# Compression weights with both parts side by side: one 512-column product per row of weights

## The chip, the cores and the metric

The kernel runs on one core of a Trainium2 chip. The metric is the device time of one execution in microseconds (us). The profile of one execution gives the busy time of the engines: PE (TensorE matmuls; PEld its weight loads), DVE (VectorE), ACT (ScalarE), POOL (GpSimd) and SP (SyncE, which issues the loads).

## The reference

A decoder trunk of two layers on 256 positions of 2048 features, all in float32: first a layer of dilated sliding-window attention, then a layer of sparse attention with compressed, selected and sliding-window branches, each followed by a squared-ReLU MLP and a gated per-layer embedding. What matters here is the compression that the second layer's first branch needs. Windows of 32 positions, 16 apart (15 of them), of the raw keys and the raw values of 4 groups go through a small MLP:

```python
def compress_blocks(blocks, pe, w1, w2):
    """blocks: (B, n_cmp, L, G, dh) -> (B, n_cmp, G, dh) via MLP with intra-block position enc."""
    B, n, L, G, dh = blocks.shape
    z = (blocks + pe[None, None, :, None, :]).transpose(0, 1, 3, 2, 4).reshape(B, n, G, L * dh)
    return jax.nn.gelu(z @ w1) @ w2
```

With L = 32 and dh = 128, `w1` is 4096 x 256, once for keys and once for values; there are 15 x 4 rows of `z` (padded to 64).

## The kernel before, in words

All weights stream from HBM once, in chunks of 128 partitions x 1024 float32 (512 KB), 873 of them in a fixed order. A chunk goes through three steps before PE uses it. `load` (L186) brings it into one of 4 `raw` buffers by a DMA on SP. `copy` (L198) rounds it on ACT to the matmul's reduced format, into a `whi` tile of 6. `sub` (L204) subtracts that on DVE from the raw chunk and keeps the rest as `wlo`, one of 5. A product with both parts is then nearly a full float32 product. Activations are split into two parts in the same way.

`Program` holds the steps in order; `Program.run` writes out each engine's instructions by hand in this order for chunk `at`: loads as far as `raw` buffers go (a buffer is free when the chunk four earlier has been subtracted), the copy of chunk `at + 4`, the subtraction of chunk `at + 3`, one step of each generator that is under way (`advance`), and then the chunk's matmuls. Each engine runs its instructions in that order. So on ACT the copy of chunk n+1 stands ahead of anything issued with the subtraction of chunk n.

The stage around the change comes after the key and value projections (`raw_quad`, `key_quad`). `compress("k")` has 8 chunks of `w_c1`, and `both` zips them with the 8 chunks of `value_unit("vs")`: compression chunk, value chunk, and so on. Then `compress("v")` is zipped with `value_unit("vw")`. That makes 32 chunks, from about 1388 to 1450 us.

- A chunk of `value_unit` (through `token_major`, L418 to L420) is 12 products of 512 columns.
- A compression chunk holds 4 x 128 rows of `w1`, 256 columns each. `z` (its two parts beside each other: 2 x 4 groups x 16 windows = 128 columns) is the stationary operand; it meets the 256 columns of `whi` (L938) and then of `wlo` (L939). All go into one accumulator of 128 x 256, whose upper and lower 64 rows belong to the two parts of `z`.
- `z_group` makes `z` for two chunks at a time: sums on DVE (`zf`, L914), rounding on ACT (L919), the rest on DVE (L922).
- `gelu` follows the eighth chunk. ACT copies the accumulator to `et` (L949). PE adds upper and lower rows with the stationary operand `pair`, two identities under each other (L955, a float32 matmul). Squares, tanh, transposes (L973) and the second weight (L989, L1018) come after, in steps between the next chunks.

In the value half DVE and ACT also split the next layer's activations (`xa`, L293 and L297). After the stage come one chunk of gate weights (`w_g`) and the query chunks (`w_q`, L327 and L329).

Of the kernel before, what the change touches and what calls it, by code (L numbers as in the profile page):

```python
# [10 lines left out]
F32 = mybir.dt.float32  # L11
# [4 lines left out]
P = 128  # L16
D = 2048
T = 256
# [23 lines left out]
def f32(ap):  # L42
    return ap.bitcast(F32)


class Program:
# [9 lines left out]
        self.steps, self.active, self.waiting, self.after = [], [], [], []  # L56

    def op(self, fn):
        self.steps.append((None, fn))

    def chunk(self, src, fn):
        self.steps.append((src, fn))

    def collect(self, fn):
        kept, self.steps = self.steps, []
# [32 lines left out]
            pass  # L98

    def run(self, load, copy, sub):  # L100
        srcs = [s for s, _ in self.steps if s is not None]
        raw, hi, lo = {}, {}, {}
        loaded = at = copied = subbed = 0
        for src, fn in self.steps:
            if src is None:
                g = fn()
                if g is not None:
                    self.begin(g)
                continue
            starting = at < KT // 2  # L110
            if starting:
                self.advance()
            ahead = max(0, min(SPLIT_AHEAD, at - KT // 2 + 2))
            while loaded < len(srcs) and loaded <= at + DMA_AHEAD:
                if loaded >= RAW_BUFS and loaded - RAW_BUFS >= subbed:
                    break
                raw[loaded] = load(loaded, srcs[loaded])
                loaded += 1
            while copied < loaded and copied <= at + ahead + (ahead > 0):
                hi[copied] = copy(copied, raw[copied])  # L120
                copied += 1
            while subbed < copied and subbed <= at + ahead:
                lo[subbed] = sub(subbed, raw.pop(subbed), hi[subbed])
                subbed += 1
            if not starting:
                self.advance()
            self.waiting += fn(hi.pop(at), lo.pop(at)) or []
            self.finish_tensor()
            at += 1
        self.until(lambda: not self.active and not self.waiting)  # L130
# [3 lines left out]
def kernel(ctx: ExitStack, tc: tile.TileContext, a: dict, out: bass.AP):  # L134
    nc = tc.nc
    ctx.enter_context(tc.manual_schedule())
    prog = Program()
# [4 lines left out]
    tmp = ctx.enter_context(tc.tile_pool(name="tmp", bufs=2))  # L142
# [15 lines left out]
    def bank():  # L158
        return pspool.tile([P, 512], F32, tag="mm", name="mm", bufs=4)
# [14 lines left out]
    pair = const.tile([P, 64], F32, name="pair")  # L174
# [16 lines left out]
    def pieces(n):  # L191

        return [slice(0, CH // 2), slice(CH // 2, CH)] if n < 2 else [slice(0, CH)]

    def copy(n, t):
        hi = wpool.tile([P, CH], F32R, tag="hi", name="whi", bufs=HI_BUFS)
        for c in pieces(n):
            nc.scalar.copy(hi[:, c], t[:, c])  # L198
        return hi

    def sub(n, t, hi):
        lo = wpool.tile([P, CH], F32R, tag="lo", name="wlo", bufs=LO_BUFS)
        for c in pieces(n):
            nc.vector.tensor_sub(lo[:, c], t[:, c], f32(hi)[:, c])  # L204
        return lo
# [700 lines left out]
    def z_group(n, b):  # L906

        prog.until(lambda: ready.get("r" + n) == GB)
        raw, pe, z = zt["r" + n], zt["pe_" + n], zt["z", b % 2]
        zf = cur["C"].tile([P, GB, 15, 8], F32, tag="zf", name="zf", bufs=2)  # L910
        part = list(raw.ap[0])
        win = bass.AP(tensor=raw.tensor, offset=raw.offset + 8 * b, ap=[part, [T, GB], [16, 15], [1, 8]])
        for g in range(GB):
            nc.vector.tensor_add(zf[:, g], win[:, g],  # L914
                                 pe[:, None, 8 * b:8 * b + 8].to_broadcast([P, 15, 8]))
        yield
        h4, l4 = (z[:, :, i].rearrange("p l g n -> p g n l")[:, :, :15, :] for i in range(2))
        for g in range(GB):
            nc.scalar.copy(h4[:, g], zf[:, g])  # L919
        yield  # L920
        for g in range(GB):
            nc.vector.tensor_sub(l4[:, g], zf[:, g], f32(h4[:, g]))  # L922
        ready["z", n, b] = True

    def compress(n, ring, then):

        st = []
        for c in range(8):
            def step(hi, lo, c=c):
                b = c // 2  # L930
                prog.until(lambda: ("z", n, b) in ready)
                z = zt["z", b % 2]
                if c == 0:
                    st.append(ring()[:, :256])
                for i in range(4):
                    zl = z[:, 4 * (c % 2) + i].rearrange("p a g n -> p (a g n)")
                    cols = slice(i * 256, (i + 1) * 256)
                    nc.tensor.matmul(st[0], zl, hi[:, cols], start=c == 0 and i == 0, stop=False)  # L938
                    nc.tensor.matmul(st[0], zl, lo[:, cols], start=False, stop=c == 7 and i == 3)  # L939
                return [gelu(n, st[0])] if c == 7 else []  # L940
            prog.chunk(a["w_c1"][(0 if n == "k" else 8) + c], step)
            if c % 2 == 1:
                m, b = (n, c // 2 + 2) if c < 5 else (then, c // 2 - 2)
                if m:
                    prog.op(lambda m=m, b=b: z_group(m, b))

    def gelu(n, ps):
        s = tmp.tile([P, T], F32, tag="et", name="et", bufs=7)
        nc.scalar.copy(s, ps)  # L949
        yield  # L950
        if n == "k":
            yield
        yield "tensor"
        y = bank()[:64, :256]
        nc.tensor.matmul(y, pair, s, start=True, stop=True)  # L955
        yield
        t = tmp.tile([64, T], F32, tag="et", name="et", bufs=7)
        u = tmp.tile([64, T], F32, tag="et", name="et", bufs=7)
        nc.scalar.activation(t, y, AF.Square)
        yield  # L960
        nc.vector.tensor_scalar(t, t, 0.044715, 1.0, op0=ALU.mult, op1=ALU.add)
        nc.vector.tensor_mul(t, y, t)
        yield
        nc.scalar.activation(t, t, AF.Tanh, scale=math.sqrt(2.0 / math.pi))
        yield
        nc.vector.scalar_tensor_tensor(u, t, 1.0, y, op0=ALU.add, op1=ALU.mult)
        yield
        if n == "k":
            yield
        yield "tensor"  # L970
        ps = bank()
        for k in range(2):
            nc.tensor.transpose(ps[:, k * 64:(k + 1) * 64], u[:, k * P:(k + 1) * P], ident[:64, :64])  # L973
        yield
        if n == "k":
            uT = cur["B"].tile([P, P], F32, name="uT", tag="uT", bufs=1)
            nc.scalar.copy(uT, ps[:, :P])
        else:
            uT = cur["B"].tile([P, 8, 3, 16], F32, name="uT3")
            nc.scalar.copy(uT, ps[:, :P].rearrange("p (b n) -> p b n", n=16)[:, :, None, :]  # L980
                           .to_broadcast([P, 8, 3, 16]))
        yield
        yield "tensor"
        yield from (comp_k(uT) if n == "k" else comp_v(uT))

    def comp_k(uT):
        ps = bank()
        for k in range(2):
            nc.tensor.matmul(ps[:64, :DH], uT[:, k * 64:(k + 1) * 64], zt["w2_k"][:, k, :],  # L989
                             start=k == 0, stop=k == 1)  # L990
        yield
        kc = cur["B"].tile([64, DH], F32, name="kc")
        nc.scalar.mul(kc, ps[:64, :DH], 0.5)
        yield
        w = cur["B"].tile([64, 32], F32, name="kcr")
        nc.vector.tensor_mul(w[:, :16], kc[:, 16:32], zt["rcS"][:, :16])
        nc.vector.tensor_mul(w[:, 16:], kc[:, :16], zt["rcS"][:, 16:])
        nc.vector.tensor_mul(kc[:, :32], kc[:, :32], zt["rcC"])
        nc.vector.tensor_add(kc[:, :32], kc[:, :32], w)
        yield  # L1000
        yield
        yield "tensor"
        ps = bank()
        nc.tensor.transpose(ps[:, :64], kc, ident[:64, :64])
        yield
        for g in range(GB):
            nc.scalar.copy(kt(g, 0)[:, :16], ps[:, 16 * g:16 * g + 16])
        yield
        for g in range(GB):
            nc.vector.tensor_sub(kt(g, 1)[:, :16], ps[:, 16 * g:16 * g + 16], f32(kt(g, 0)[:, :16]))  # L1010
        ready["kc"] = True
# [28 lines left out]
    def both(f, g):  # L1040
# [4 lines left out]
    raw_quad("rk", 0)  # L1045
    raw_quad("rv", 1, {5: [lambda: z_group("k", 0)], 6: [lambda: z_group("k", 1)]})
    both(lambda: compress("k", bank, "v"), lambda: value_unit("vs", 3))
    both(lambda: compress("v", bank, None),
         lambda: value_unit("vw", 5, {c: [lambda k=k: split_x(k, G_ATTN + 1, x_a1) for k in (2 * c, 2 * c + 1)]
# [284 lines left out]
```

## Time and profile before

| | before |
|---|---|
| median of 3 runs | 2513.16 us (2512.55 to 2513.68) |
| the profiled execution: its time | 2514.11 us |
| the profiled execution: span of the profile | 2511.3 us |
| mean granted clock of TensorE | 0.999 |
| loads of 512 KB from `w_c1` | 16, median 4.3 us from issue to landing |
| loads of 512 KB from `w_kv` | 48, median 4.3 us from issue to landing |
| matmul instructions of the compression's products (L938, L939) | 64 and 64 |

A row of the timeline has the start in us from the span's start, the length, engine, line, operation, result and operands, their shape, the number of instructions merged (x2), and in brackets the idle time before with what ended it. A merged row's length runs from the first start to the last end. PE's lengths overlap, since matmuls are pipelined: PE's pace is read from start to start. Rows of groups have busy time, mean length in ns, and the idle time ahead of them with its releasers. SPq rows are issues of loads.

### The profile page before, as it was taken

How to read it: one execution, taken by the hardware profiler on the slowest of the kernel's cores; microseconds unless marked ns; L12 is line 12 of the kernel's file. 1: busy time of each engine (PE TensorE's matmuls, PEld its weight loads, DVE VectorE, ACT ScalarE, POOL GpSimd, SP SyncE). 2: the span in 40 equal slices, each digit the busy share in tenths (PEclk: the TensorE clock that was granted, in tenths of full speed). 3: DMA queues.
4: the chain of work that ended last, by engine and by line, in shares of the span. 5: the costliest groups of instructions: out<-in, count | busy, mean ns of one | idle time of the engine just before them, and what ended most of it. 6: DMA issues, size and time to landing. Idle time of an engine off the chain costs nothing.

```text
span 2511.3 us, 36082 instructions
## 1 busy us (share of the span) xinstructions
PE 2500.4 (100%) x13497; PEld 2156.5 (86%) x13497; DVE 1662.3 (66%) x2808; ACT 1351.0 (54%) x2168; POOL 10.4 (0%) x24
## 2 busy tenths in 40 slices
PE   9999999999999999999999999999999999999998
PEld 8888888888888888888888889888888888888887
DVE  7766677865465565566787989766546556556676
ACT  6444444554454453455564788755545445445455
POOL 0000000000000000000000000000000000000000
PEclk9999999999999999999999999999999999999999
DMA  7555545556555655555565753455555655665553
GB/s 272 172 179 178 175 161 181 173 188 193 193 188 193 191 192 193 192 192 185 186 195 189 243 163 121 141 191 190 192 192 188 193 192 192 193 192 190 182 189 121
DMA packets 130111, 466.10 MB, mean 186 GB/s; under 512 B 14608, under 2 KB 15888, under 8 KB 129936
## 3 DMA queue, kind: packets, MB, share of 16 engines
q1 hardware_dynamic: 129264, 462.68, 56.6%
q8 instruction: 105, 1.72, 0.3%
q0 software_dynamic: 528, 1.07, 0.2%
q14 instruction: 70, 0.57, 0.1%
q10 hardware_dynamic: 144, 0.07, 0.0%
HBM read 461.65 MB, written 2.10 MB: 185 GB/s over the span
## 4 chain that ended last, share of the span: by engine, by line
PE 99%; DVE 0%; DMA 0%; SPq 0%; ACT 0%; issue 0%; DVEq 0%
PE mm L327 22%; PE at L327 17%; PE mm L329 11%; PE at L329 9%; PE mm L418 6%; PE mm L420 6%; PE mm L419 6%; PE at L420 5%; PE at L418 5%; PE at L419 5%; PE at L1180 0%; PE at L718 0%; PE mm L1204 0%; PE mm L938 0%; PE mm L939 0%; DMA raw<-in_w_v 0%
## 5 line engine op out<-in xcount | busy, mean ns | idle before, releaser
L204 DVE TENSOR_TENSOR wlo<-raw,whi 128x1024 fp32r<-128x1024 f32 (+1 forms) x875 | 1065.7, 1219 | 634.3 <-PE at L420 131.5
L198 ACT CAST whi<-raw 128x1024 fp32r<-128x1024 f32 (+1 forms) x875 | 919.8, 1052 | 880.4 <-PE at L327 198.9
L327 PE MATMUL mm<-xa,whi 128*128 128x512 f32 x2176 | 756.4, 396 | 0.0
L329 PE MATMUL mm<-xa,wlo 128*128 128x256 f32 x2176 | 587.9, 278 | 0.0
L327 PE MATMUL at<-xa,whi 128*128 128x512 f32 x1648 | 573.7, 393 | 0.0
L327 PEld LDWEIGHTS mm<-xa,whi 128*128 128x128 f32 x2176 | 401.4, 188 | 85.1 <-issue 0.4
L329 PE MATMUL at<-xa,wlo 128*128 128x256 f32 x1648 | 458.5, 278 | 0.0
L329 PEld LDWEIGHTS mm<-xa,wlo 128*128 128x128 f32 x2176 | 409.4, 188 | 9.7
L327 PEld LDWEIGHTS at<-xa,whi 128*128 128x128 f32 x1648 | 308.7, 187 | 70.0
L329 PEld LDWEIGHTS at<-xa,wlo 128*128 128x128 f32 x1648 | 310.2, 188 | 0.1
L418 PE MATMUL at<-whi,h 128*128 128x512 f32 x512 | 199.5, 390 | 0.0
L418 PE MATMUL mm<-whi,h 128*128 128x512 f32 x512 | 199.4, 389 | 0.0
L419 PE MATMUL mm<-whi,h 128*128 128x512 f32 x512 | 199.2, 389 | 0.0
L420 PE MATMUL mm<-wlo,h 128*128 128x512 f32 x512 | 199.2, 389 | 0.0
L420 PE MATMUL at<-wlo,h 128*128 128x512 f32 x512 | 199.2, 389 | 0.0
L419 PE MATMUL at<-whi,h 128*128 128x512 f32 x512 | 199.2, 389 | 0.0
L420 PEld LDWEIGHTS at<-wlo,h 128*128 128x128 f32 x512 | 96.1, 188 | 20.0
L420 PEld LDWEIGHTS mm<-wlo,h 128*128 128x128 f32 x512 | 96.1, 188 | 20.0
L418 PEld LDWEIGHTS mm<-whi,h 128*128 128x128 f32 x512 | 96.1, 188 | 19.9
L419 PEld LDWEIGHTS at<-whi,h 128*128 128x128 f32 x512 | 96.1, 188 | 19.8
L418 PEld LDWEIGHTS at<-whi,h 128*128 128x128 f32 x512 | 96.1, 188 | 19.8
L419 PEld LDWEIGHTS mm<-whi,h 128*128 128x128 f32 x512 | 96.1, 188 | 19.6
(315 smaller groups left out, 2529.5 us busy)
## 6 DMA issues: line engine op xcount, KB each, us to landing
raw<-in_w SPq DMA_DIRECT2D x512, 512.0 KB, 3.6
raw<-in_w_qk SPq DMA_DIRECT2D x96, 512.0 KB, 3.5
raw<-in_w_gate SPq DMA_DIRECT2D x56, 512.0 KB, 4.0
raw<-in_w_kv SPq DMA_DIRECT2D x48, 512.0 KB, 4.3
raw<-in_w_v SPq DMA_DIRECT2D x46, 512.0 KB, 3.6
raw<-in_w_q SPq DMA_DIRECT2D x32, 512.0 KB, 4.4
raw<-in_w_oB SPq DMA_DIRECT2D x32, 512.0 KB, 3.5
raw<-in_w_oA SPq DMA_DIRECT2D x16, 512.0 KB, 3.5
```

The lines of the kernel that those rows point to most:

```text
L198: nc.scalar.copy(hi[:, c], t[:, c])
L204: nc.vector.tensor_sub(lo[:, c], t[:, c], f32(hi)[:, c])
L327: nc.tensor.matmul(ps, hi[:, col:col + P], rhs, start=first, stop=False)
L329: nc.tensor.matmul(ps[:, :T], lo[:, col:col + P], rhs[:, :T], start=False, stop=last)
L418: nc.tensor.matmul(st[j], xh, wh, start=k == 0, stop=False)
L419: nc.tensor.matmul(st[j], xl, wh, start=False, stop=False)
L420: nc.tensor.matmul(st[j], xh, wl, start=False, stop=k == KT - 1)
```

## The change

A compression chunk is split into two other tiles. Of a chunk's four rows of weights, `whi` takes the first two with both parts side by side (256 columns rounded, 256 columns rest, twice), `wlo` the other two likewise. One product of 512 columns per row of weights then goes into an accumulator of 128 x 512, whose two halves belong to the two parts of the weights. `chunk` gets a width for such chunks (256), which `run` hands to `copy` and `sub`. `copy` makes the rounded part of the first tile; `sub` makes the rounded part of the second on ACT, and then both rests on DVE, each instruction 512 elements. `gelu` copies both halves of the accumulator (two copies of 256 columns on ACT) and adds all four quarters with two `pair` matmuls into one accumulator. All other chunks are split as before.

```diff
-                hi[copied] = copy(copied, raw[copied])
+                hi[copied] = copy(copied, raw[copied], wide[copied])
...
-                lo[subbed] = sub(subbed, raw.pop(subbed), hi[subbed])
+                lo[subbed] = sub(subbed, raw.pop(subbed), hi[subbed], wide[subbed])
...
+    def beside(t, raw, j, w):
+
+        return raw.rearrange("p (j i c) -> p j i c", j=2, c=w)[:, j], t.rearrange("p (i a c) -> p i a c", a=2, c=w)
+
+    def copy(n, t, wide):
         hi = wpool.tile([P, CH], F32R, tag="hi", name="whi", bufs=HI_BUFS)
+        if wide:
+            src, dst = beside(hi, t, 0, wide)
+            nc.scalar.copy(dst[:, :, 0, :], src)
+            return hi
...
+    def sub(n, t, hi, wide):
         lo = wpool.tile([P, CH], F32R, tag="lo", name="wlo", bufs=LO_BUFS)
+        if wide:
+            halves = [beside(both, t, j, wide) for j, both in enumerate((hi, lo))]
+            src, dst = halves[1]
+            nc.scalar.copy(dst[:, :, 0, :], src)
+            for src, dst in halves:
+                nc.vector.tensor_sub(dst[:, :, 1, :], src, f32(dst[:, :, 0, :]))
+            return lo
...
-            def step(hi, lo, c=c):
+            def step(*both, c=c):
...
-                    st.append(ring()[:, :256])
+                    st.append(ring())
                 for i in range(4):
                     zl = z[:, 4 * (c % 2) + i].rearrange("p a g n -> p (a g n)")
-                    cols = slice(i * 256, (i + 1) * 256)
-                    nc.tensor.matmul(st[0], zl, hi[:, cols], start=c == 0 and i == 0, stop=False)
-                    nc.tensor.matmul(st[0], zl, lo[:, cols], start=False, stop=c == 7 and i == 3)
+                    nc.tensor.matmul(st[0], zl, both[i // 2][:, i % 2 * 512:(i % 2 + 1) * 512],
+                                     start=c == i == 0, stop=c == 7 and i == 3)
...
     def gelu(n, ps):
-        s = tmp.tile([P, T], F32, tag="et", name="et", bufs=7)
-        nc.scalar.copy(s, ps)
+        s = [tmp.tile([P, T], F32, tag="et", name="et", bufs=7) for _ in range(2)]
+        for i in range(2):
+            nc.scalar.copy(s[i], ps[:, i * T:(i + 1) * T])
...
-        nc.tensor.matmul(y, pair, s, start=True, stop=True)
+        for i in range(2):
+            nc.tensor.matmul(y, pair, s[i], start=i == 0, stop=i == 1)
```

More of the change, by code (lines that the diff above doesn't have):

```diff
@@ L58, in op, with chunk @@
     def op(self, fn):
-        self.steps.append((None, fn))
-    def chunk(self, src, fn):
-        self.steps.append((src, fn))
+        self.steps.append((None, fn, None))
+    def chunk(self, src, fn, wide=None):
+        self.steps.append((src, fn, wide))
     def collect(self, fn):
@@ L100, in run @@
     def run(self, load, copy, sub):
-        srcs = [s for s, _ in self.steps if s is not None]
+        srcs = [s for s, _, _ in self.steps if s is not None]
+        wide = [w for s, _, w in self.steps if s is not None]
         raw, hi, lo = {}, {}, {}
         loaded = at = copied = subbed = 0
-        for src, fn in self.steps:
+        for src, fn, _ in self.steps:
             if src is None:
@@ L193, in pieces @@
         return [slice(0, CH // 2), slice(CH // 2, CH)] if n < 2 else [slice(0, CH)]
-    def copy(n, t):
+    def beside(t, raw, j, w):
+        return raw.rearrange("p (j i c) -> p j i c", j=2, c=w)[:, j], t.rearrange("p (i a c) -> p i a c", a=2, c=w)
+    def copy(n, t, wide):
         hi = wpool.tile([P, CH], F32R, tag="hi", name="whi", bufs=HI_BUFS)
+        if wide:
+            src, dst = beside(hi, t, 0, wide)
+            nc.scalar.copy(dst[:, :, 0, :], src)
+            return hi
         for c in pieces(n):
@@ L199, in copy @@
         return hi
-    def sub(n, t, hi):
+    def sub(n, t, hi, wide):
         lo = wpool.tile([P, CH], F32R, tag="lo", name="wlo", bufs=LO_BUFS)
+        if wide:
[5 more added lines that the diff above has]
+            return lo
         for c in pieces(n):
@@ L933, in step @@
                 if c == 0:
-                    st.append(ring()[:, :256])
+                    st.append(ring())
                 for i in range(4):
                     zl = z[:, 4 * (c % 2) + i].rearrange("p a g n -> p (a g n)")
-                    cols = slice(i * 256, (i + 1) * 256)
-                    nc.tensor.matmul(st[0], zl, hi[:, cols], start=c == 0 and i == 0, stop=False)
-                    nc.tensor.matmul(st[0], zl, lo[:, cols], start=False, stop=c == 7 and i == 3)
+                    nc.tensor.matmul(st[0], zl, both[i // 2][:, i % 2 * 512:(i % 2 + 1) * 512],
+                                     start=c == i == 0, stop=c == 7 and i == 3)
                 return [gelu(n, st[0])] if c == 7 else []
-            prog.chunk(a["w_c1"][(0 if n == "k" else 8) + c], step)
+            prog.chunk(a["w_c1"][(0 if n == "k" else 8) + c], step, 256)
             if c % 2 == 1:
```

## The prediction

> **What bounds the kernel now.** I read the page's top, its chain of work, then the same stage in the windows view, in the waits and in the timeline.
>
> ```profile
> span 2511.3 us, 36082 instructions
> PE 2500.4 (100%) x13497; PEld 2156.5 (86%) x13497; DVE 1662.3 (66%) x2808; ACT 1351.0 (54%) x2168; POOL 10.4 (0%) x24
> PE 99%; DVE 0%; DMA 0%; SPq 0%; ACT 0%; issue 0%; DVEq 0%
> ...
> 1388.40:1418.30 29.90, 29.81 (x162) 25.68 (x161) 26.64 (x51) 19.49 (x31) 0.00 (x0) 1.00 0.77 248
> 1418.30:1448.00 29.70, 29.70 (x161) 24.38 (x160) 29.40 (x56) 26.63 (x49) 0.00 (x0) 1.00 0.80 261
> ```
>
> TensorE is the bound: 99% of the chain that ended last is PE. So an edit gains only by giving PE less to do, and loses as soon as PE waits. The two window rows are the stage that is edited: the compression of the keys, then that of the values, each zipped chunk by chunk with a value unit. Columns are length, then busy time of PE, PEld, DVE, ACT, POOL, then clock, DMA share and GB/s. PE still never idles there (29.81 of 29.90, 29.70 of 29.70), at full clock, but everything that feeds it is near its limit: in the second half DVE has 0.3 us free of 29.70, ACT 3.1 us.
>
> ```profile
> SPq L186 <- DVE wlo L204: 31.3, 18, 4.3
> ...
> ACT whi L198 <- DMA raw<-in_w_kv: 7.4, 8, 1.8
> ...
> PEld mm L955 <- ACT et L949: 0.4, 1, 0.4
> ```
>
> These are the waits between 1388 and 1452 us (total, times, longest). Loads wait for DVE (18 times), ACT waits for loads (8 times): with four `raw` buffers this is a ring. A load starts when the subtraction of the chunk four earlier is done, ACT copies what has landed, DVE subtracts, the next load starts. The last row is where the ring already touches PE: the value side's `pair` matmul (L955) waits for ACT.
>
> **The products.** 128 products of 256 columns become 64 of 512.
>
> ```profile
> 1392.43 0.29 PE L938 MATMUL mm<-whi,z 128*128 128x256 f32 x1
> ...
> 1393.39 0.39 PE L418 MATMUL at<-whi,xa 128*128 128x512 f32 x1
> ...
> 1396.14 0.29 PE L938 MATMUL mm<-whi,z 128*128 128x256 f32 x1
> ...
> 1403.57 0.29 PE L938 MATMUL mm<-whi,z 128*128 128x256 f32 x1
> ```
>
> A compression chunk takes PE 1393.39 − 1392.43 = 0.96 us for 8 products of 256, that is 0.120 each; the 12 products of 512 of the next value chunk take 1396.14 − 1393.39 = 2.75, 0.229 each. Four wide ones are 0.92: columns count, not instructions. Saved: 16 × 0.04 = 0.64 us at the very most. [...] Two chunk pairs take PE 1403.57 − 1396.14 = 7.43 us here; that is the pace the ring must keep.
>
> **The splits.** The compression's `hi` tile now takes weight columns 0 to 511, both parts side by side, `lo` the other 512. ACT makes two copies of 512 in place of one of 1024, DVE two subtractions of 512 in place of one.
>
> ```profile
> L204 DVE TENSOR_TENSOR wlo<-raw,whi 128x1024 fp32r<-128x1024 f32 x871 | 1063.1, 1222 | 632.9 <-PE at L420 131.5 <-PE mm L420 130.0 <-PE mm L329 119.4
> L198 ACT CAST whi<-raw 128x1024 fp32r<-128x1024 f32 x871 | 917.4, 1054 | 879.0 <-PE at L327 198.9 <-PE mm L419 198.0 <-PE mm L327 196.3
> ...
> L204 DVE TENSOR_TENSOR wlo<-raw,whi 128x512 fp32r<-128x512 f32 x4 | 2.6, 691 | 1.5 <-ACT whi L198 1.4
> L198 ACT CAST whi<-raw 128x512 fp32r<-128x512 f32 x4 | 2.4, 617 | 1.3 <-DMA raw<-in_w_v 1.3
> ```
>
> DVE: 2 × 0.691 − 1.222 = +0.16 us per compression chunk; ACT: 2 × 0.617 − 1.054 = +0.18. The destinations are now runs of 256 with gaps, which no row shows; I take the price of the plain 512, since nothing in it but the step of the address differs. Two back to back may overlap a little at their ends, so +0.08 to +0.16 for DVE.
>
> The order matters more than the size. The second copy is issued with the subtraction, and the program issues the copy of chunk n+1 before the subtraction of chunk n. So on ACT it stands behind `whi` of the next chunk, and that waits for its load. On DVE the second subtraction waits for this copy, and behind it stand the value chunk's `wlo`, `zf` and `z`; SP's next loads wait for those. One turn of the ring, two chunk pairs long, from the end of a value chunk's `wlo`:
>
> ```profile
> 1396.97 0.33 SPq L186 DMA_DIRECT2D raw<-in_w_kv  x1
> ...
> 1401.78 1.05 ACT L198 CAST whi<-raw 128x1024 fp32r<-128x1024 f32 x1 [0.68 <-DMA raw<-in_w_kv]
> ...
> 1412.44 0.33 SPq L186 DMA_DIRECT2D raw<-in_w_kv  x1
> ...
> 1417.24 1.05 ACT L198 CAST whi<-raw 128x1024 fp32r<-128x1024 f32 x1 [0.90 <-DMA raw<-in_w_kv]
> ...
> 1390.06 2.00 ACT L198 CAST whi<-raw 128x1024 fp32r<-128x1024 f32 x2
> ...
> 1410.06 2.35 DVE L204 TENSOR_TENSOR wlo<-raw,whi 128x1024 fp32r<-128x1024 f32 x2
> ```
>
> - `wlo` ends 1410.06 + 2.35 = 1412.41, the load goes out 1412.44: 0.03
> - issue to the start of `whi`: 4.81 and 4.80, both with ACT waiting for the DMA: 4.80
> - two `whi` in a row take 2.00, so the second copy starts 2.00 − 1.05 = 0.95 after
> - the second copy itself 0.62, a hand-over of 0.03 as at the load
> - the second subtraction 0.69; then the value chunk's `wlo`, 2.35 − 1.22 = 1.13 further on
>
> Sum 8.25 us per turn against PE's 7.43: the ring falls behind by 0.82. Between the end of the first copies and the stage's middle there are 8 pairs, 4 turns: 3.3 us. Before the change the own copy of a chunk was enough, and the two subtractions ran without that wait.
>
> A start-up lag comes first. `whi` of the second chunk starts at 1390.06; today the compression chunk's `wlo` runs from 1390.54 to 1391.76, 1.70 after it.
>
> ```profile
> 1390.54 1.22 DVE L204 TENSOR_TENSOR wlo<-raw,whi 128x1024 fp32r<-128x1024 f32 x1
> ...
> 1418.42 0.29 PE L938 MATMUL mm<-whi,z 128*128 128x256 f32 x1
> ...
> 1446.65 0.39 PE L938 MATMUL mm<-whi,z 128*128 128x256 f32 x1
> ```
>
> After: 0.95 + 0.62 + 0.03 + 0.69 = 2.29, so 0.6 later. In the second half PE's own pace is slower, (1446.65 − 1418.42) / 7 × 2 = 8.07 per two pairs, because small fp32 products stand in between; there the ring's 8.25 hardly loses, but DVE, which has nothing free, gets 8 × 0.16 = 1.3 us more. Lateness at the end of the stage: 0.6 + 3.3 + 1.3 = 5.2 us.
>
> **What it costs PE.** Splits are done ahead of use, so part of the lateness is covered at first.
>
> ```profile
> 1431.59 1.21 DVE L204 TENSOR_TENSOR wlo<-raw,whi 128x1024 fp32r<-128x1024 f32 x1
> ...
> 1435.43 0.40 PE L418 MATMUL at<-whi,xa 128*128 128x512 f32 x1
> ...
> 1443.31 1.23 DVE L204 TENSOR_TENSOR wlo<-raw,whi 128x1024 fp32r<-128x1024 f32 x1
> ...
> 1444.57 0.33 SPq L186 DMA_DIRECT2D raw<-in_w_q  x1
> ...
> 1449.19 1.05 ACT L198 CAST whi<-raw 128x1024 fp32r<-128x1024 f32 x1 [0.39 <-DMA raw<-in_w_q]
> 1450.14 0.37 ACT L949 COPY et<-mm 128x256 f32<-128x256 f32 x1
> ...
> 1450.23 0.39 PE L420 MATMUL at<-wlo,xa 128*128 128x512 f32 x1
> ...
> 1450.56 0.65 PE L955 MATMUL mm<-et,pair 128*64 128x256 f32 x2
> 1451.14 0.74 PE L327 MATMUL mm<-xa,whi 128*128 128x512 f32 x2
> ```
>
> The cover is smallest at 1432.80, 2.6 us before use at 1435.43. It doesn't help at the end: the last `wlo` of the stage ends at 1444.54, releases the load at 1444.57, whose `whi` waits for it till 1449.19, behind which ACT makes `et`, ready at 1450.51; PE was through with its last product at 1450.23 + 0.23 = 1450.46. Nothing is spare, so PE's start at L955 moves by the whole lateness. Stalls that PE takes earlier, once the 2.6 us are used up, are part of that sum and not added; the 0.64 us that the products save and the first `pair` matmul added only change how long PE waits here.
>
> The second `pair` matmul on the value side comes on top. One takes 1451.14 − 1450.56 = 0.58 with its switch; between two halves of its two passes, 2 × 0.23, and this, I take 0.5. Its second copy of `et`, about 0.3, hides under the first matmul.
>
> Sum: 5.2 + 0.5 = 5.7 us. The profiled execution took 2514.11 us (span 2511.3 and 2.8 around it), 0.95 above the median of the runs; on it 2519.8, on the median of 2513.16 us 2518.9.
>
> **The rivals.** (1) Loads land sooner when the ring turns slower, and nothing is late: not slower.
>
> ```profile
> 1391.82 0.33 SPq L186 DMA_DIRECT2D raw<-in_w_c  x1
> ...
> 1395.37 1.05 ACT L198 CAST whi<-raw 128x1024 fp32r<-128x1024 f32 x1 [0.42 <-DMA raw<-in_w_c]
> ```
>
> A load that goes out alone takes 3.55 us to its copy; with that the turn is 8.25 − 1.25 = 7.00, under PE's 7.43. It decides at 4.80 − 0.82 = 3.98. The start-up lag is then made good, 0.5 for the `pair` matmul and some of DVE's 1.3 stay, 0.64 is saved: 2513.2 to 2514.4, say 2513.8. Against it: a value chunk's load always follows the compression chunk's by one subtraction, so two share the queues. [...] The rows, 3.55 alone and 4.80 in pairs, speak against it. Chance 0.22.
>
> (2) The lateness grows further: ACT, with 3.1 us free in the second half, gets 8 × 0.18 = 1.4 us more and the waits for loads ahead of DVE's second subtraction; if half of each turn's new wait (0.95 + 0.62) also comes on DVE's full queue there, 4 × 0.8 = 3.2 us more: 2522.1. It decides when DVE, at 99% busy, can't fill that wait. Chance 0.14.
>
> (3) Faster by over 0.2%: PE would have to lose 5 of the 16 × 0.96 = 15.4 us of its compression products. The columns stay, so I leave it 0.03.
>
> **How the numbers follow.** The forecast case has 0.61 and runs from 2516.5 to 2521. 0.2% is 5.0 us, about what a measurement of this kernel can tell from no change; the bound lies at 2518.2, so some two thirds of the case, 0.42, and rival 2 are slower: 0.56. The rest of it and rival 1 are 0.41, faster 0.03. The range takes in rival 1's middle and rival 2's, 2513.8 to 2522.5.
>
> **What would show it.** In the changed profile: a compression chunk's four products 0.92 us apart; 512-wide copies of 0.62 and subtractions of 0.69; DVE waiting for ACT's second copy at nearly every compression chunk, ACT waiting for value loads; turns of 8 us and more in the key half; PE idle for some us ahead of the value side's `pair` matmul and perhaps ahead of some products before; everything later shifted by the same amount. I am wrong if value loads reach their copy in under 4 us, if the shift at that matmul is under 2 us, or if PE stalls after it grow.

## The result, and the profile after

The changed kernel takes 2519.96 us (median of 8 runs, 2518.08 to 2522.79) against 2513.42 us (median of 8, 2512.55 to 2514.59): 1.0027 times the time before, 95% interval 1.0017 to 1.0037. It is slower, by 6.5 us. The ratios here and below leave out one run of 12492 us, of the first experiment's kernel. The profiled execution took 2518.87 us, its span is 5.5 us longer than before.

The top of the page of the changed kernel, and its chain of work:

```profile
span 2516.8 us, 35992 instructions
...
PE 2501.3 (99%) x13437; PEld 2154.4 (86%) x13437; DVE 1663.3 (66%) x2824; ACT 1352.6 (54%) x2186; POOL 10.4 (0%) x24
...
PE 96%; DVE 1%; DMA 1%; issue 1%; ACT 0%; SPq 0%; DVEq 0%; ACTq 0%
```

PE is busy nearly as long as before (2501.3 against 2500.4 us), but the span has grown by 5.5 us: most of the added time is waiting. In the chain, PE has lost 3% to DVE, the DMA and issue. The stage in the windows (length, then PE, PEld, DVE, ACT, POOL, clock, DMA share, GB/s) shows where:

```profile
1388.40:1418.30 29.90, 29.35 (x128) 23.79 (x127) 25.83 (x56) 18.86 (x36) 0.00 (x0) 1.00 0.68 229
1418.30:1448.00 29.70, 28.16 (x122) 21.46 (x122) 26.72 (x59) 25.67 (x54) 0.00 (x0) 1.00 0.73 238
```

PE, which had a gap of 0.09 us here, now idles 0.55 and 1.54 us. No engine is busier in these windows: DVE fell from 29.40 to 26.72 us in the second half, the DMA share from 0.80 to 0.73. That is a chain of waits, not an engine that has become too slow. From the compression's first product to the first product of the gate's chunk the stage takes 74.05 us, before 68.47; from there to the end both kernels take the same time.

The waits of the changed kernel from 1388 to 1460 us (total, times, longest):

```profile
ACT whi L207 <- DMA raw<-in_w_kv: 9.3, 10, 2.0
DVE wlo L217 <- ACT wlo L215: 6.2, 9, 1.3
...
PE mm L972 <- ACT et L965: 2.8, 1, 2.8
...
PE mm L990 <- DVE et L983: 0.9, 1, 0.9
...
PE at L434 <- DVE et L351: 0.5, 1, 0.5
...
PE mm L1006 <- ACT uT L994: 0.4, 1, 0.4
...
PE at L436 <- DVE wlo L220: 0.2, 1, 0.2
```

L207 is now the copy of an ordinary chunk, L215 the copy of a compression chunk's second tile, L217 that chunk's two subtractions, L220 the subtraction of an ordinary chunk, L972 the `pair` matmul. The second row is new: DVE waits for the second copy. The five PE rows add up to 4.8 us, 2.8 of it ahead of the value side's `pair` matmul. The groups by form give this wait over all 16 compression chunks, the two split ahead of 1388 us among them: 9.8 us (busy, mean ns | idle before, and its cause). It came at 11 of the 16; at the other five the second copy was ready in time.

```profile
L217 DVE TENSOR_TENSOR wlo<-raw,wlo 128x512 fp32r<-128x512 f32 x16 | 11.0, 688 | 9.8 <-ACT wlo L215 9.8
...
L215 ACT CAST wlo<-raw 128x512 fp32r<-128x512 f32 x16 | 9.8, 615 | 0.0
```

One turn of the ring, from the timeline:

```profile
1402.24 0.33 SPq L187 DMA_DIRECT2D raw<-in_w_kv  x1
...
1406.57 1.06 ACT L207 CAST whi<-raw 128x1024 fp32r<-128x1024 f32 x1 [1.22 <-DMA raw<-in_w_kv]
1407.53 0.62 ACT L215 CAST wlo<-raw 128x512 fp32r<-128x512 f32 x1
...
1406.84 0.68 DVE L217 TENSOR_TENSOR whi<-raw,whi 128x512 fp32r<-128x512 f32 x1
1408.18 0.69 DVE L217 TENSOR_TENSOR wlo<-raw,wlo 128x512 fp32r<-128x512 f32 x1 [0.65 <-ACT wlo L215]
1408.79 1.22 DVE L220 TENSOR_TENSOR wlo<-raw,whi 128x1024 fp32r<-128x1024 f32 x1
...
1410.03 0.33 SPq L187 DMA_DIRECT2D raw<-in_w_kv  x1
```

The first copy's tile is subtracted at 1406.84, and DVE could go on. But the second copy (1407.53) stands on ACT behind the next chunk's copy (1406.57), which waits 1.22 us for its load. DVE stands till 1408.18, its value chunk's `wlo` ends at 1410.01, and only then does the next load go out.

At the end of the stage:

```profile
1448.41 1.21 DVE L220 TENSOR_TENSOR wlo<-raw,whi 128x1024 fp32r<-128x1024 f32 x1
...
1449.65 0.33 SPq L187 DMA_DIRECT2D raw<-in_w_q  x1
...
1454.18 1.04 ACT L207 CAST whi<-raw 128x1024 fp32r<-128x1024 f32 x1 [0.70 <-DMA raw<-in_w_q]
1455.13 0.64 ACT L965 COPY et<-mm 128x256 f32<-128x256 f32 x2
...
1452.36 0.39 PE L436 MATMUL at<-wlo,xa 128*128 128x512 f32 x1
...
1455.55 1.08 PE L972 MATMUL mm<-et,pair 128*64 128x256 f32 x4 [2.80 <-ACT et L965]
1456.56 0.73 PE L343 MATMUL mm<-xa,whi 128*128 128x512 f32 x2
```

The last `wlo` ends at 1449.62 where it ended at 1444.54; load, `whi` and `et` follow as before, and PE starts the `pair` matmul at 1455.55 instead of 1450.56, 5.0 us later.

### The profile page after: what moved, and what is told of

Read it like the earlier page. It is cut to its first block, busy times and chain, and to the rows that moved or that the text cites. A ratio compares the mean times of both kernels' runs of the same rounds, so it can differ in the third digit from the quotient of the medians.

```text
span 2516.8 us, 35992 instructions
## 1 busy us (share of the span) xinstructions
PE 2501.3 (99%) x13437; PEld 2154.4 (86%) x13437; DVE 1663.3 (66%) x2824; ACT 1352.6 (54%) x2186; POOL 10.4 (0%) x24
## 4 chain that ended last, share of the span: by engine, by line
PE 96%; DVE 1%; DMA 1%; issue 1%; ACT 0%; SPq 0%; DVEq 0%; ACTq 0%
PE mm L343 22%; PE at L343 17%; PE mm L345 11%; PE at L345 8%; PE mm L436 6%; PE mm L435 6%; PE mm L434 6%; PE at L436 5%; PE at L434 5%; PE at L435 5%; DMA raw<-in_w_kv 1%; PE at L1197 0%; DVE wlo L220 0%; PE at L734 0%; PE mm L1221 0%
## 5 line engine op out<-in xcount | busy, mean ns | idle before, releaser
L220 DVE TENSOR_TENSOR wlo<-raw,whi 128x1024 fp32r<-128x1024 f32 (+1 forms) x859 | 1046.2, 1219 | 628.7 <-PE at L436 131.5
L207 ACT CAST whi<-raw 128x1024 fp32r<-128x1024 f32 (+1 forms) x859 | 903.3, 1052 | 876.6 <-PE mm L343 199.4
L434 PE MATMUL at<-whi,h 128*128 128x512 f32 x512 | 199.5, 390 | 0.0
L434 PE MATMUL mm<-whi,h 128*128 128x512 f32 x512 | 199.4, 389 | 0.0
L436 PE MATMUL mm<-wlo,h 128*128 128x512 f32 x512 | 199.3, 389 | 0.0
L436 PE MATMUL at<-wlo,h 128*128 128x512 f32 x512 | 199.2, 389 | 0.0
L436 PEld LDWEIGHTS mm<-wlo,h 128*128 128x128 f32 x512 | 96.1, 188 | 20.0
L434 PEld LDWEIGHTS mm<-whi,h 128*128 128x128 f32 x512 | 96.1, 188 | 20.0
L434 PEld LDWEIGHTS at<-whi,h 128*128 128x128 f32 x512 | 96.1, 188 | 19.9
L436 PEld LDWEIGHTS at<-wlo,h 128*128 128x128 f32 x512 | 96.1, 188 | 19.9
```

Source lines behind the costliest of these rows:

```text
L434: nc.tensor.matmul(st[j], xh, wh, start=k == 0, stop=False)
L436: nc.tensor.matmul(st[j], xh, wl, start=False, stop=k == KT - 1)
```

## The experiments

My theory: the whole loss is the place of the second copy on ACT, behind a copy that waits for its load, in a ring that has only four buffers. Rivals: the smaller instructions (size), the `pair` matmul's early place, and the wide products themselves.

**Second tile's copy ahead of the next chunk's copy.** In `run`, with `sub` unchanged:

```diff
+            while subbed < copied and subbed <= at + ahead:
+                lo[subbed] = sub(subbed, raw.pop(subbed), hi[subbed], wide[subbed])
+                subbed += 1
             while copied < loaded and copied <= at + ahead + (ahead > 0):
```

> The changed kernel with one thing moved: the second tile's copy (and both subtractions) of chunk n are issued ahead of the copy of chunk n+1, so on ACT it no longer stands behind a copy that waits for the next load. Same instructions, same sizes, same products. Order theory (the ring of raw buffers turns too slowly because the second copy waits for the next load): the last subtraction of the stage is late by 1 to 2 us instead of 5.1, PE's gap before the value side's pair matmul falls from 3.2 to under 1.5 us, time 2514.5 to 2516.5. Size theory (the lateness comes from two 512-wide instructions where one of 1024 was, on an ACT and a DVE that had no room): nothing changes, 2519 to 2521. Product theory (the wide products and the second pair matmul): nothing changes either.

2513.8 us, ratio 1.0001 (0.9992 to 1.0010): the loss is gone with all else in place, more fully than the 2514.5 to 2516.5 expected. The last subtraction of the stage is late by 0.7 us, where 1 to 2 were expected. Its waits and windows:

```profile
ACT whi L210 <- DMA raw<-in_w_kv: 5.2, 6, 1.4
...
DVE wlo L220 <- ACT wlo L218: 1.0, 1, 1.0
...
PE mm L975 <- ACT et L968: 0.5, 1, 0.5
```

```profile
1388.40:1418.30 29.90, 29.79 (x132) 24.17 (x131) 28.16 (x61) 21.50 (x43) 0.00 (x0) 1.00 0.78 252
1418.30:1448.00 29.70, 29.70 (x130) 22.92 (x129) 28.23 (x61) 25.79 (x52) 0.00 (x0) 1.00 0.78 254
```

DVE's wait for the second copy falls from 9 times to one, PE is as busy as before the change, and its wait ahead of the `pair` matmul falls from 2.8 to 0.5 us.

**The order alone.** The kernel before, its narrow products and one `pair` matmul kept; only a compression chunk's split is made in the changed kernel's order:

```diff
+        if wide:
+            nc.scalar.copy(hi[:, two[0]], t[:, two[0]])
+            return hi
...
+        if wide:
+            nc.scalar.copy(hi[:, two[1]], t[:, two[1]])
+            for c in two:
+                nc.vector.tensor_sub(lo[:, c], t[:, c], f32(hi)[:, c])
+            return lo
```

> The kernel before with its narrow products, its accumulator of 256 columns and one pair matmul; only the split of the compression's chunks is changed: the first half of whi is copied where it was, the second half with the subtraction, behind the next chunk's copy, and DVE subtracts in two halves. Order theory: the lateness at the end of the stage is 4.5 to 5.5 us as in the changed kernel, and the time is 2518 to 2519.5 (less by the second pair matmul, 0.5). Product theory: 2513 to 2515.

2519.91 us, ratio 1.0024 (1.0015 to 1.0033). Its waits:

```profile
DVE wlo L212 <- ACT whi L210: 6.0, 9, 0.9
...
PE mm L966 <- ACT et L960: 2.6, 1, 2.6
```

The same two waits in nearly the same size (6.2 and 2.8 in the changed kernel), without a single wide product. The last `wlo` ends at 1449.90 us, 5.36 late, as expected. The time is 0.4 us above the expected 2518 to 2519.5; the slow clock of which this section tells last is in its profile too.

**The size alone.** The same kernel with both 512-column copies made at once in `copy`:

```diff
+        if wide:
+            for c in two:
+                nc.scalar.copy(hi[:, c], t[:, c])
+            return hi
```

> The kernel before with its narrow products; the compression's chunks are copied in two halves of 512, both at once where the one copy was, and subtracted in two halves. So the sizes and counts of the changed kernel without its order. Order theory: only DVE's and ACT's additions remain, 1.3 us or less, 2513.5 to 2515. Size theory: 4 to 5 us late, 2517.5 to 2519.

2513.31 us, ratio 0.9999 (0.9990 to 1.0008). Its second half in the windows:

```profile
1418.30:1448.00 29.70, 29.70 (x160) 24.39 (x159) 29.45 (x63) 26.70 (x52) 0.00 (x0) 1.00 0.80 260
```

DVE is as full as before and PE doesn't wait. Its first pair of subtractions shows why so little is paid:

```profile
1390.41 1.28 DVE L212 TENSOR_TENSOR wlo<-raw,whi 128x512 fp32r<-128x512 f32 x2
```

Two subtractions in a row take 1.28 us, 0.06 more than one of 1024, not 0.16: they overlap by 0.1 us. So the size costs no time that can be measured here.

**A fifth raw buffer.** If the loss is the ring's, one more buffer should end it with the order unchanged. A first kernel took the room from the `whi` tiles:

```diff
-RAW_BUFS, HI_BUFS, LO_BUFS = 4, 6, 5
+RAW_BUFS, HI_BUFS, LO_BUFS = 5, 5, 5
```

> The changed kernel with five raw buffers instead of four (and five whi tiles instead of six, for the room). Order theory: a load may start one chunk sooner, so a turn of the ring covers five chunks; 8.25 us for 5 chunks is 6.6 for 4, less than PE's 7.4, and the lateness goes but for what DVE has to do in the second half: 2514.5 to 2517. If instead DVE's or ACT's own work is what falls behind, an earlier load doesn't help: 2519 to 2521. If five whi tiles are too few, PE waits appear outside this stage too.

2530.30 us, ratio 1.0067 (1.0054 to 1.0079). The miss is of the experiment: with five `whi` tiles the kernel loses time all along, 3.3 us against the changed kernel by 1282 us, ahead of this stage, and more behind it. Ahead of the value side's `pair` matmul PE's gap was 0.32 us, which agrees with the theory but can't carry it. So the room was taken elsewhere, `es` from 4 to 2 buffers and `sq` from 3 to 2, once with the fifth raw buffer and once without:

```diff
-RAW_BUFS, HI_BUFS, LO_BUFS = 4, 6, 5
+RAW_BUFS, HI_BUFS, LO_BUFS = 5, 6, 5
```

> The changed kernel with five raw buffers and all six whi tiles; the room comes from fewer small tiles (es two instead of four, sq two instead of three), whose own price the next run has. Order theory: with a load starting one chunk sooner the ring keeps up, the gap before the value side's pair matmul is under 1 us, and it is 3 to 5 us faster than the next run. If the copy's place costs its time without the ring, no difference to the next run.

> The changed kernel with four raw buffers as it is, and only the fewer small tiles of the run before (es two, sq two). Price of the smaller pools alone: 2519 to 2523, with the gap of 3 us before the value side's pair matmul.

With five 2513.62 us, ratio 1.0000 (0.9991 to 1.0009); with four 2519.82 us, ratio 1.0022 (1.0014 to 1.0031). The smaller `es` and `sq` change nothing that shows; the fifth buffer gives back all of it, 6.2 us where 3 to 5 were expected. Waits with five, then with four:

```profile
DVE wlo L217 <- ACT wlo L215: 2.2, 4, 1.1
```

```profile
DVE wlo L217 <- ACT wlo L215: 6.3, 8, 1.1
...
PE mm L972 <- ACT et L965: 2.0, 1, 2.0
```

With a load in hand, ACT waits less for one (8 times and 6.8 us for the stage's loads, against 11 times and 13.1 us with four buffers), so the second copy waits less behind it. PE doesn't wait at the `pair` matmul there.

**The `pair` matmul one chunk later.** The stall at L972 is only where the lateness comes out. Here the value side's `gelu` yields twice, as the key side's does:

```diff
         yield
-        if n == "k":
-            yield
+        yield
         yield "tensor"
```

> The changed kernel with the value side's pair matmul issued one chunk later (the key side's has this distance already), so that PE has one query chunk, 2.8 us, to do while ACT still waits. If the 3.2 us gap there is only missing cover: the gap falls below 0.6 us, the other stalls (0.7 us at the first value chunk, some 2.5 us ahead of the small matmuls of the value half) stay, and the time falls by 2.4 to 3.2 us, to 2516.5 to 2517.8. If the lateness of the splits holds PE in any case, PE waits at the query chunk's first products instead and the time stays at 2519 to 2521. If PE's clock falls after a gap of 3 us, as the spread of the changed kernel's runs (2518.1 to 2522.8) may mean, the runs lie closer together than that.

2517.84 us, ratio 1.0017 (1.0008 to 1.0026). Of the 6.5 us 2.0 are gained, a little less than the 2.4 to 3.2 expected. The long wait goes, the rest comes out at other places: PE still waits 0.9 us for `et` (L982) and 0.55 at the first value chunk, and now 0.47 at the attention behind the query chunks (L1097); the wait at a value chunk's L436 grows from 0.2 to 0.5. The 11 runs lie closer together, from 2517.40 to 2519.88, as was expected if PE's clock falls after a long wait. So the early place makes the lateness visible but isn't its cause.

**The best of it.** Order mended and `pair` matmul one chunk later, both as above, and the accumulator's halves added on ACT and DVE ahead of a single `pair` matmul:

```diff
     def gelu(n, ps):
-        s = [tmp.tile([P, T], F32, tag="et", name="et", bufs=7) for _ in range(2)]
-        for i in range(2):
-            nc.scalar.copy(s[i], ps[:, i * T:(i + 1) * T])
+        s = sum_halves(ps)
```

> The changed kernel's layout and wide products, with the second tile's copy issued ahead of the next chunk's copy, the value side's pair matmul one chunk later, and the accumulator's halves added by ACT and DVE (one pair matmul as before). The order theory leaves no wait and PE saves 16 x 0.04 = 0.64 us of products: 2512.5 to 2513.5, at most 0.6 us better than before. If the wide products save nothing, 2513.5 to 2514.

2513.97 us, ratio 1.0001 (0.9992 to 1.0010). The stage takes 67.78 us in its profile against 68.47 before, but the 0.7 us don't show in the times, which miss the 2512.5 to 2513.5 expected. The profiled execution, the longest of its 11 runs, was already 1.7 us behind at the stage's first product (1390.09 against 1388.38). What the wide products can bring at best is below what a measurement of this kernel can tell.

**What the median has beyond the span.** The profiled execution is 5.5 us longer in its span, the median 6.5. A filled gap tells whether PE's wait does something to the clock: eleven products of 128 x 128 into unused columns, ahead of the value side's `pair` matmuls.

```diff
-        y = bank()[:64, :256]
+        b = bank()
+        y = b[:64, :256]
+        for _ in range(11 if n == "v" else 0):
+            nc.tensor.matmul(b[:, 256:384], ones, ones, start=True, stop=True)
```

> The changed kernel, with eleven more products of the 128 x 128 ones, written to columns of the pair's bank that nobody reads, issued ahead of the value side's pair matmuls, so that PE works through part of the 3.2 us for which it waits there; no wait is taken away. Theory: the wait costs its own 3 us in every run, and in some runs more, because the granted clock falls after it; with PE kept at work the wait stays, the runs gather at 2518 to 2519.6 with a granted clock of 0.999, and the median is about 2518.8. Rival: the runs above 2520 of the changed kernel have nothing to do with this gap; then they lie from 2518 to 2523 as before, with a median of about 2520 and clocks of 0.997 to 0.999. If the extra products themselves come in the way, the time is up to 1 us above either.

2519.38 us (2518.85 to 2520.61), ratio 1.0024 (1.0014 to 1.0034): between the two expected medians, but all 9 clocks at 0.999. To tell it apart, the changed kernel and the filled one were timed once more side by side.

> The changed kernel, as it is, timed on the same chip as the one with extra products. If the runs above 2520 come of the clock after PE's 3 us wait, they are here again: a third to half of the runs above 2520, up to 2522, some with a granted clock of 0.997 or 0.998, median about 2519.8. If they were a matter of the chip on which the first runs were made, all runs lie from 2518 to 2520 with 0.999, like those of the kernel with extra products.

> The kernel with eleven extra products in the wait, on the same chip as the changed kernel itself. Clock theory: median 0.3 to 1 us below that of the changed kernel, no run above 2521, clocks 0.999. Rival: both are alike within 0.3 us in median and in highest run.

The changed kernel: 2520.48 us (8 runs, 2518.96 to 2521.91), ratio 1.0029 (1.0018 to 1.0039), clocks of 0.998 in 4 runs. The filled one: 2519.33 us (10 runs, 2518.60 to 2520.17), ratio 1.0024 (1.0015 to 1.0033), 0.999 in all. That is 1.15 us less in the median, near the 0.3 to 1 expected. This time the profile of the changed kernel caught the cause. Its windows and products behind the wait:

```profile
1452.00:1456.00 4.00, 1.34 (x6) 0.81 (x5) 3.79 (x9) 3.38 (x11) 0.00 (x0) 0.95 0.89 301
1456.00:1460.00 4.00, 4.00 (x13) 2.55 (x13) 3.73 (x6) 4.00 (x8) 0.00 (x0) 0.62 0.86 317
```

```profile
1455.75 1.97 PE L972 MATMUL mm<-et,pair 128*64 128x256 f32 x4 [2.66 <-ACT et L965]
1457.65 1.22 PE L343 MATMUL mm<-xa,whi 128*128 128x512 f32 x2
1458.67 0.57 PE L345 MATMUL mm<-xa,wlo 128*128 128x256 f32 x2
1459.08 0.62 PE L343 MATMUL mm<-xa,whi 128*128 128x512 f32 x2
```

In the order-only kernel the same window behind its wait of 2.62 us, and then the same window in the first profile of the changed kernel, where the wait was 2.80 us:

```profile
1456.00:1460.00 4.00, 4.00 (x14) 2.76 (x14) 4.00 (x7) 4.00 (x8) 0.00 (x0) 0.60 0.91 314
```

```profile
1456.00:1460.00 4.00, 4.00 (x22) 3.14 (x21) 3.73 (x7) 4.00 (x8) 0.00 (x0) 1.00 0.88 317
```

The same products in the first profile of the changed kernel, and in the filled kernel's second (where each of the eleven products is two instructions):

```profile
1457.12 0.40 PE L345 MATMUL mm<-xa,wlo 128*128 128x256 f32 x2
1457.36 0.64 PE L343 MATMUL mm<-xa,whi 128*128 128x512 f32 x2
```

```profile
1453.05 2.62 PE L973 MATMUL mm<-ones 128*128 128x128 f32 x22
1456.05 1.08 PE L975 MATMUL mm<-et,pair 128*64 128x256 f32 x4 [0.39 <-ACT et L965]
...
1457.87 0.63 PE L343 MATMUL mm<-xa,whi 128*128 128x512 f32 x2
```

From the `pair` matmuls to the third group of products: 1459.08 − 1455.75 = 3.33 us in a window whose mean granted clock is 0.62, against 1457.36 − 1455.55 = 1.81 at 1.00, and 1.82 in the filled kernel. So in some executions the wait costs 1.5 us more, after it has ended.

## Why the prediction was right, and where its terms were off

The forecast was 2518.9 us, slower; measured were 2519.96, slower, inside the range. The range, 2513.8 to 2522.5, would have held rival 1's time too, so the number alone proves little. The mechanism is the one forecast: the order alone costs nearly all of it (6.3 us), the size nothing that can be measured, and mending the order or the ring each gives it back. By its steps:

| step | forecast | measured |
|---|---|---|
| products of a compression chunk | 0.92 us | 0.94 |
| start-up lag | 0.6 | 0.86 |
| turn of the ring, key half | 8.25 | 7.79 in the turn above, 8.1 mean of the 6 between the `wlo` of 1392.87 and 1421.23 us |
| lateness of `wlo` eight pairs on, in mid-stage | 0.6 + 3.3 = 3.9 | 3.9 |
| lateness of the last `wlo` | 5.2 | 5.08 |
| second `pair` matmul | 0.5 | 0.43 |
| span | +5.7 | +5.5 |
| median | +5.7 | +6.5 |

The lateness is read from the same subtractions, of the kernel before (L204) and of the changed one (L220):

```profile
1392.01 1.22 DVE L204 TENSOR_TENSOR wlo<-raw,whi 128x1024 fp32r<-128x1024 f32 x1
...
1422.57 1.22 DVE L204 TENSOR_TENSOR wlo<-raw,whi 128x1024 fp32r<-128x1024 f32 x1
```

```profile
1392.87 1.22 DVE L220 TENSOR_TENSOR wlo<-raw,whi 128x1024 fp32r<-128x1024 f32 x1
...
1426.50 1.21 DVE L220 TENSOR_TENSOR wlo<-raw,whi 128x1024 fp32r<-128x1024 f32 x1
```

- **Start-up.** 0.86, not 0.6 (1.0 counting that the changed kernel was 0.17 us ahead before the stage). From `whi` to the end of the second subtraction it is the 2.29 us forecast (1390.33 to 1392.62); the other 0.27 is that this `whi` itself starts at 1390.33 instead of 1390.06. And PE took a stall that no step had: 0.5 us at the first value chunk (L434 waits for `et`, L351), because DVE, behind the first compression chunks' split, frees an accumulator late. A fifth raw buffer doesn't end this one: it is there in that kernel too (0.5 us).
- **The turn.** The load to copy took 4.33 us in the turn shown, where 4.80 was taken from two turns of before; the other parts, 0.96, 0.65, 0.61 and 1.24, are as forecast. The 4.80 was a choice: the six value loads of before from 1393.26 to 1412.44 us took 4.32 to 6.33, 5.1 on the mean. The six of the changed kernel from 1394.12 to 1414.56 us took 4.33 to 5.29, 4.6 on the mean. So loads do reach their copy a little sooner when the ring turns slower, as rival 1 had it, but in the key half not under 3.98, where that rival decides. One load in the value half did (3.92, issued at 1432.29), which the forecast had named as a sign of being wrong; one alone didn't mend the ring.
- **The two halves.** The key half came out: eight pairs on, the lateness is 1427.71 − 1423.79 = 3.9 us. (It goes up and down with the kernel before: one pair earlier it is 2.9, where the kernel before itself waited 0.39 us for ACT.) The value half added 1.2 us, near the 1.3, but not for the reason given, so this part of the number is luck. DVE's longer work adds 0.07 us to the lateness at each compression chunk there, not 0.16: the kernel with the size alone pays 0.06 where two subtractions follow each other, and loses no time. Behind the eighth pair five such chunks are left, not eight, so this makes 0.4 us of the 1.2. The rest comes at the last two compression chunks, where DVE again waits for the second copy (0.18 and 0.50 us). That is rival 2's mechanism, in a small part of the 3.2 us that it was priced at on top of the 1.3. DVE's wait came at 11 of 16 chunks, not at nearly every one.
- **No cover at the end.** Right: PE's start at the `pair` matmul moved by 5.0 us for 5.08 of lateness. Of this 2.0 had been taken in earlier stalls, as the text allowed.
- **The products.** 0.64 us at most was the bound; a chunk's four products are 0.94 apart (1392.68 to 1393.62), so 16 × 0.02 = 0.3 us is saved.

```profile
1392.68 0.64 PE L953 MATMUL mm<-whi,z 128*128 128x512 f32 x2
...
1393.62 0.39 PE L434 MATMUL at<-whi,xa 128*128 128x512 f32 x1
```

- **The median.** The step that was missing is the clock after the wait (0.62 on the mean from 1456 to 1460 us): 1.5 us in the execution whose profile caught it, and about 1 us of the median, by the 1.15 us between the changed and the filled kernel.

Rival 3, faster, had its condition in the products and falls with them.

## What to carry to other kernels

When an edit splits one step of a pipeline in two, look at where the second half lands in each engine's queue: here a copy of 0.6 us in each of 16 chunks cost 6.5 us in all, because it stood behind an instruction that waits for a load. Follow the ring of buffers once around, with every wait in it, and compare the turn with the bound engine's pace; a few tenths per turn add up till the next place without cover. If a turn is too long, issue the dependent half ahead of the waiting instruction or add a buffer; either was enough.

## What was not expected of the hardware

A wait of PE of under 3 us was at times followed by a lower granted clock. In the changed kernel's second profile, where the wait was 2.66 us, the mean was 0.95 from 1452 to 1456 us, 0.62 from 1456 to 1460 and 1.00 from 1460 to 1464; in the order-only kernel's, with 2.62 us, it was 0.97, 0.60 and again 1.00 behind it. Two products of 256 columns took 0.41 us in the stretch of 0.62 (1458.67 to 1459.08) against 0.24 in the changed kernel's first profile (1457.12 to 1457.36). It was so in some executions and not in others of the same kernel. The mean clock of a run is only a rough sign of it: it was 0.997 or 0.998 in 9 of 16 runs of the changed kernel and 0.999 in all 19 with PE kept at work in the gap, but the order-only kernel's profiled run, with the slow stretch, has 0.999 too.

Why some executions escape isn't shown. The length of the wait alone doesn't decide it: with the longest of the three, 2.80 us in the changed kernel's first profile, the mean clock was 1.00 from 1452 to 1464 us. The kernel with five `raw` and five `whi` tiles has 0.94 from 1388.40 to 1418.30 us, the window that holds its wait of 2.3 us (PE at L434 for `et`, L351).
